# SwiGLU operands in two sets of tiles, six prepared weight blocks kept for the second half, output weight sums formed in the input stage

## The chip, the cores and the metric

The kernel runs on one core of one Trainium2 chip. TensorE (PE in the profile) multiplies matrices, VectorE (DVE), ScalarE (ACT) and GpSimd (POOL) work element by element, and SyncE (SP) issues the transfers between the main memory and the on-chip memory (SBUF). PE writes to eight PSUM banks, which DVE and ACT read. Every engine works through its own list of instructions strictly in that list's order and waits by semaphores for the others. The metric is the device time of one execution in microseconds; lower is better.

## The reference

One encoder layer works on 1280 tokens (1024 of a prompt and 256 of a sample) of width 1024: a mixer (differential attention beside a gated linear recurrence, the LRU), cross-attention into 2 x 256 memory tokens, and a SwiGLU of inner width 2816, each followed by a residual and a layer norm. The change lies in the SwiGLU, and in where some of its sums are formed:

```python
def swiglu(x, ffn_w_in, ffn_w_out):
    g, u = jnp.split(x @ ffn_w_in, 2, axis=-1)
    return (jax.nn.silu(g) * u) @ ffn_w_out

x = layer_norm(alpha*x + swiglu(x, ffn_w_in, ffn_w_out), ln3_g, ln3_b)
# mixer, the side products: sigmoid(g_attn) * (attn_out @ p_attn) + sigmoid(g_lru) * (lru_out @ p_lru)
```

## The kernel before

All matrix products are made of split operands: a float32 value is kept as a high part (a rounded copy) and a low part (the value minus the high part), and a product takes three matmuls: high by high, high by low, low by high. A **split** thus costs a copy on ACT and a subtraction on DVE or POOL (`split`, line 192).

The stages follow each other in time: input products with the LRU and the rotation of queries and keys (0 to 632 us of the span); attention with "filler" products between its steps (632 to 1395), the last of which are the side products with `p_lru`; `p_attn` and the mixer output (1395 to 1623); cross-attention (1623 to 1928); the SwiGLU (from 1928 on).

**First SwiGLU product.** Tokens are taken in two halves of 640. For each half 22 **units** f run, one for each block of 128 inner columns. A unit multiplies the gate block and the up block of weights by the tokens with a 7-product Strassen scheme (`strassen`, lines 359 to 391): seven products of 12 matmuls (4 steps of 3) of 320 columns, 84 matmuls in all, each product into one PSUM bank, and eight small evacuations (one on ACT, seven on DVE). The 7 weight operands of a unit are gate and up sub-blocks and four sums of them, each split in two: `pair_ops` (lines 328 to 349) loads both blocks (`raw`), forms the sums on DVE and POOL and splits. The gate pair goes to the pool `WT` (4 buffers of `wh` and `wl`), the other five pairs to `ws`, which has 5 buffers of each part, so one set. `P_ORDER` (line 357) uses the operands in the order 0, 5, 1, 6, 4, 2, 3; `pair_ops` writes operand 3 first of the five. Units 0 to 3 are **reloaded**: their operands were prepared during cross-attention and stand in main memory (`fpd`), and 14 transfers of 256 KB bring them in. I call the other 18 units **fresh**. The token operands `xb` are seven split combinations, one set for the half (`combine`, line 1129).

**Second SwiGLU product.** It is a Strassen scheme over inner halves and output halves, seven out-products (`out_product`, line 1266) of 11 steps of 15 matmuls of 512 columns. Product 0 runs between the two halves, product 1 after the second half, then 4, 5, 2, 6 and 3. The left sums are formed in `sums` (second half, one DVE operation for units below 11, three from 11 on) and stored to `sd`; the weight sums in `weight_sums` (first half, units 1 to 11, four DVE operations) are stored to `td`. `inner` and `inner2` load a step's two sources and split them.

**Order.** A scheduler lays out each engine's list from the order in which the code is written, pool sizes and priorities (`high_priority` with a negative offset puts work later). SP's list holds all loads and stores, so that a store which waits for its source also holds back the loads behind it. Fillers are drawn by `fill(done)` as attention proceeds; all their products share one PSUM bank (`ps_m`, line 681).

```python
while filled[0] < upto:                       # fill, line 722
for j in range(5): ... combine(j, xf, ...)    # after out_product(0, ...), lines 1301 to 1306
```

Of the kernel before, what the change touches and what calls it, by code (L numbers as in the profile page):

```python
# [9 lines left out]
F32 = mybir.dt.float32  # L10
# [22 lines left out]
FDB = 1  # L33
MSTB = 4
# [10 lines left out]
RELOAD = 4  # L45
PREP = 100
# [48 lines left out]
WSB = 5  # L95
# [45 lines left out]
def encoder_layer_kernel(ctx: ExitStack, tc: tile.TileContext, i, y_out):  # L141
# [11 lines left out]
    def f32(ap):  # L153
        return ap.bitcast(F32)
# [28 lines left out]
    fpd = dt_("fpd", [RELOAD, 7, 2, 128, 512])  # L183
# [3 lines left out]
    sd = dt_("sd", [4, NF // 2, 128, 640])  # L187
    td = dt_("td", [NF // 2, 128, 4, 512])
    SA = {4: 0, 5: 1, 6: 2, 2: 3}
# [240 lines left out]
    with ExitStack() as es:  # L430
# [170 lines left out]

        steps = [(k, b) for b in range(8) for k in "xy"]
# [16 lines left out]
        for n, (kind, b) in enumerate(steps):  # L619
# [46 lines left out]
    with ExitStack() as es:  # L666
# [16 lines left out]
        def fillers():  # L683
# [14 lines left out]
            for c0, n in (CHUNKS[2], CHUNKS[0], CHUNKS[1]):  # L698
# [18 lines left out]
        anchor = [None]  # L717
# [103 lines left out]
        done = 0.0  # L821
        for u in range(len(units) + VLAG):
# [23 lines left out]
            fill(done)  # L846
# [276 lines left out]
    with ExitStack() as es:  # L1123
# [47 lines left out]
        with ExitStack() as es1:  # L1171
# [6 lines left out]
            def reloaded(f):  # L1178
                if f == 0:
                    gs = [RW.tile([128, 1024], F32, tag="raw", name="raw").bitcast(F32R) for t in "hl"]  # L1180
                else:
                    gs = [WT.tile([128, 1024], F32R, tag="w" + t, name="w" + t) for t in "hl"]
                u = [tuple(ws.tile([128, 512], F32R, tag=t, name="s" + t) for t in "hl") for _ in range(5)]
                w = [tuple(g[:, c * 512:c * 512 + 512] for g in gs) for c in range(2)] + u
                for n, _ in P_ORDER:
                    for m in range(2):
                        SP.dma_start(f32(w[n][m]), fpd[f, n, m])
                return w

            def hidden(half_, f):  # L1190
                w = reloaded(f) if f < RELOAD else pair_ops(i["ffn_in"][f], i["ffn_in"][NF + f], [ws.tile([128, 512], F32R, tag=t, name="s" + t) for _ in range(5) for t in "hl"], rx, E_W, E_S)
# [11 lines left out]
            def sums(f, h):  # L1203
                def summand(src):
                    z = sp.tile([128, 640], F32, tag="z", name="hz")
                    SP.dma_start(z, src)
                    return z

                def put(n, z):
                    SP.dma_start(sd[SA[n], f % NK], z)  # L1210

                if f < NK:
                    z = summand(hd[0, f])
                    V.tensor_tensor(z, z, h, ALU.subtract)
                    put(6, z)
                    return
                k = f - NK
                z = summand(hd[1, k])
                V.tensor_tensor(z, z, h, ALU.add)  # L1219
                put(4, z)  # L1220
                y = summand(hd[0, k])
                V.tensor_tensor(y, z, y, ALU.subtract)
                put(5, y)
                z = summand(hd[0, f])
                V.tensor_tensor(z, z, y, ALU.subtract)
                put(2, z)


            def weight_sums(k):
                lo, hi, sa, sb = (rx.tile([128, 2, 512], F32, tag="raw", name="so") for _ in range(4))  # L1230
                SP.dma_start(lo, i["ffn_out"][k].rearrange("p (c n) -> p c n", c=2))
                SP.dma_start(hi, i["ffn_out"][NK + k].rearrange("p (c n) -> p c n", c=2))
                t1, t2, t3, t4 = sa[:, 0], sa[:, 1], sb[:, 0], sb[:, 1]
                V.tensor_tensor(t1, lo[:, 1], lo[:, 0], ALU.subtract)
                V.tensor_tensor(t2, hi[:, 1], t1, ALU.subtract)
                V.tensor_tensor(t3, hi[:, 1], lo[:, 1], ALU.subtract)
                V.tensor_tensor(t4, hi[:, 0], t2, ALU.subtract)
                SP.dma_start(td[k, :, 0:2, :], sa)
                SP.dma_start(td[k, :, 2:4, :], sb)
# [4 lines left out]
            def sources(n, k):  # L1244
                a = ASRC[n](k) if n in ASRC else sd[SA[n], k]
                b = BSRC[n](k) if n in BSRC else td[k, :, TB[n], :]
                return a, b
# [6 lines left out]
            def inner(n, k):  # L1254
                a, b = sources(n, k)
                return (parts(a, RW.tile([128, 1024], F32, tag="raw", name="raw")[:, :640], *(WT.tile([128, 1024], F32R, tag="w" + t, name="a" + t)[:, :640] for t in "hl")),
                        parts(b, rx.tile([128, 2, 512], F32, tag="raw", name="rb")[:, 0], *(ws.tile([128, 512], F32R, tag=t, name="b" + t) for t in "hl")))
# [30 lines left out]
            for half_ in range(2):  # L1288
                for f in range(NF):
# [6 lines left out]
                    if half_:  # L1296
                        sums(f, h)
                    elif 1 <= f <= NK:
                        weight_sums(f - 1)
                if half_ == 0:  # L1300
                    out_product(0, evac0, inner)
                    operands()
                    for j in range(5):
                        xf = rx.tile([128, 8, 128], F32, tag="raw", name="xf")
                        SP.dma_start(xf, x2t[:, :, j * 128:j * 128 + 128].rearrange("k p t -> p k t"))
                        combine(j, xf, rx.tile([128, 4, 4, 64], F32, tag="raw", name="tt"))
            out_product(1, evac1, inner)

        esx.close()
        with ExitStack() as es1:  # L1310
            ap_ = pool(es1, "a2", NK)
            rp = pool(es1, "raw2", 3)
            zp = pool(es1, "yb", 5)
            xt = pool(es1, "xt", 3)
            st = pool(es1, "stG", 2)
            gp = pool(es1, "gbF", 1)
            gt = gp.tile([128, D], F32, tag="g", name="lng")
            bt = gp.tile([128, D], F32, tag="b", name="lnb")
            SP.dma_start(gt, i["ln3_g"].partition_broadcast(128))
            SP.dma_start(bt, i["ln3_b"].partition_broadcast(128))  # L1320
            yb = []

            def inner2(n, k):
                a, b = sources(n, k)
                return (parts(a, rp.tile([128, 640], F32, tag="a", name="ra"), *(ap_.tile([128, 640], F32R, tag="a" + t, name="a" + t) for t in "hl")),
                        parts(b, RW.tile([128, 1024], F32, tag="raw", name="rb")[:, :512], *(ap_.tile([128, 512], F32R, tag="b" + t, name="b" + t) for t in "hl")))
# [9 lines left out]
            def normed(half_, p, y):  # L1336
                end = half_ == 1 and p == 4
                full = half_ == 1 and p >= 3
                with tc.high_priority(offset=0 if half_ else -LNP):
# [104 lines left out]
```

## Time and profile before

| | us |
|---|---|
| median of 3 runs | 2880.44 |
| lowest and highest | 2877.9, 2885.94 |
| profiled execution, whole | 2877.44 |
| its span, first to last instruction | 2875.6 |
| PE busy in the span | 2725.6 (95%) |
| DVE, ACT, POOL busy | 1753.2, 1205.3, 757.1 |
| mean granted clock of PE, share of full speed | 0.981 |

Busy time of PE counts matmuls that overlap, so that the length of a stretch, divided by the length of the same work without a wait, tells more. Idle time of the other engines matters only where PE waits for them.

### The profile page before, as it was taken

Reading aid. Unit: us, or ns where it says so; the run is one execution under the profiler, and the core shown is the slowest. Engines: PE = TensorE matmul, PEld = TensorE weight load, DVE = VectorE, ACT = ScalarE, POOL = GpSimd, SP = SyncE. Lnnn points to the kernel's source line nnn. Section 1 sums busy time; section 2 is a strip of 40 time slices with the busy share of each in tenths; the row PEclk is TensorE's granted clock in tenths of the full one; section 3 lists DMA queues with packets and bytes.
Section 4 is the critical chain, followed back from the end, with each engine's and each line's share of the span. In section 5 each row is a group of like instructions: output and inputs, shape, how many; then the busy total and the mean of one; then the engine's idle time right before and its main releaser. Section 6 shows DMA issues by size and latency. Waiting matters only on the chain. (4 is left out here: it accounts for less than half of the span.)

```text
span 2875.6 us, 40844 instructions
## 1 busy us (share of the span) xinstructions
PE 2725.6 (95%) x15075; PEld 2403.2 (84%) x15075; DVE 1753.2 (61%) x2567; ACT 1205.3 (42%) x2046; POOL 757.1 (26%) x491
## 2 busy tenths in 40 slices
PE   9999999999999999999999999999889789889898
PEld 7888888878899888888788899779889688888787
DVE  4546766416667655654355675556986457796568
ACT  3666445326666555554120254212333323333542
POOL 0000000014355443434001000322556245552004
PEclk9999999999999999999999999999999989999999
DMA  9533545574567756647786594669743663567654
GB/s 354 201 110 119 183 155 195 171 238 135 155 207 234 235 154 219 229 143 240 271 272 209 190 315 140 213 223 338 262 134 108 221 220 129 174 220 258 206 183 161
DMA packets 334792, 583.94 MB, mean 203 GB/s; under 512 B 27264, under 2 KB 170368, under 8 KB 334592
## 3 DMA queue, kind: packets, MB, share of 16 engines
q1 hardware_dynamic: 334592, 581.33, 60.9%
q8 instruction: 119, 1.95, 0.3%
q14 instruction: 81, 0.66, 0.1%
HBM read 389.33 MB, written 191.89 MB: 202 GB/s over the span
## 5 line engine op out<-in xcount | busy, mean ns | idle before, releaser
L197 POOL TENSOR_TENSOR wl<-raw,wh 128x1024 fp32r<-128x1024 f32 x88 | 213.2, 2424 | 913.0 <-ACT wh L194 865.2
L194 ACT ACTIVATE wh<-raw 128x1024 fp32r<-128x1024 f32 (+1 forms) x224 | 224.4, 1005 | 520.7 <-PE ps L293 152.3
L364 PE MATMUL ps<-xbh,sl 128*128 128x320 f32 x880 | 278.7, 317 | 41.4 <-DVE sl L197 41.0
L362 PE MATMUL ps<-xbh,sh 128*128 128x320 f32 x880 | 277.0, 315 | 23.8 <-ACT sh L194 13.9
L527 PE MATMUL ps<-xh,wh 128*128 128x512 f32 (+1 forms) x768 | 274.4, 357 | 11.3 <-ACT xh L194 6.1
L363 PE MATMUL ps<-xbl,sh 128*128 128x320 f32 x880 | 275.2, 313 | 0.0
L528 PE MATMUL ps<-xl,wh 128*128 128x512 f32 (+1 forms) x768 | 274.0, 357 | 0.5 <-DVE xl L197 0.5
L529 PE MATMUL ps<-xh,wl 128*128 128x512 f32 (+1 forms) x768 | 273.4, 356 | 0.0
L290 PE MATMUL ps<-fh,wh 128*128 128x512 f32 (+1 forms) x704 | 258.8, 368 | 10.8 <-DVE g L712 6.3
L293 PE MATMUL ps<-fl,wh 128*128 128x512 f32 (+1 forms) x704 | 255.6, 363 | 3.2 <-DMA fl<-memd 2.5
L197 DVE TENSOR_TENSOR wl<-raw,wh 128x1024 fp32r<-128x1024 f32 (+1 forms) x136 | 153.1, 1132 | 168.3 <-ACT wh L194 155.8
L294 PE MATMUL ps<-fh,wl 128*128 128x512 f32 (+1 forms) x704 | 254.9, 362 | 0.0
L750 DVE TENSOR_REDUCE nm<-s 128x1 f32<-128x1024 f32 (+1 forms) x160 | 167.3, 1059 | 93.6 <-PE s L749 92.9
L857 POOL TENSOR_TENSOR rstd<-rstd,mhalf 128x1 f32<-128x1 f32 x30 | 37.0, 1233 | 687.5 <-DVE rstd L856 687.5
L364 PEld LDWEIGHTS ps<-xbh,sl 128*128 128x128 f32 x880 | 168.1, 191 | 49.3 <-DVE sl L197 48.8
L362 PEld LDWEIGHTS ps<-xbh,sh 128*128 128x128 f32 x880 | 168.0, 191 | 27.7 <-ACT sh L194 17.0
L752 ACT ACTIVATE e<-s,nm 128x1024 f32<-128x1024 f32 (+1 forms) x160 | 158.7, 996 | 57.8 <-DVE nm L750 55.9
L527 PEld LDWEIGHTS ps<-xh,wh 128*128 128x128 f32 x768 | 146.4, 191 | 33.4 <-ACT xh L194 6.1
L363 PEld LDWEIGHTS ps<-xbl,sh 128*128 128x128 f32 x880 | 168.1, 191 | 0.0
L528 PEld LDWEIGHTS ps<-xl,wh 128*128 128x128 f32 x768 | 146.3, 190 | 21.5 <-DVE xl L197 1.1
L529 PEld LDWEIGHTS ps<-xh,wl 128*128 128x128 f32 x768 | 146.1, 190 | 20.7
L290 PEld LDWEIGHTS ps<-fh,wh 128*128 128x128 f32 x704 | 133.3, 189 | 34.6 <-issue 4.5
(287 smaller groups left out, 7334.1 us busy)
## 6 DMA issues: line engine op xcount, KB each, us to landing
raw<-w_in SPq DMA_DIRECT2D x80, 512.0 KB
raw<-ffn_in SPq DMA_DIRECT2D x80, 512.0 KB
q<-qd SPq DMA_DIRECT2D x320, 64.0 KB
hd<-hh SPq DMA_DIRECT2D x44, 320.0 KB
hz<-hd SPq DMA_DIRECT2D x44, 320.0 KB
sd<-hz SPq DMA_DIRECT2D x44, 320.0 KB
ra<-sd SPq DMA_DIRECT2D x44, 320.0 KB
raw<-p_lru SPq DMA_DIRECT2D x24, 512.0 KB
```

The source lines that it names most:

```text
L194: S.activation(h, src, AF.Copy)
L197: leng.tensor_tensor(l, src, f32(h), ALU.subtract)
L290: ins = PE.matmul(ps, a, h, start=(k == 0), stop=False)
L293: PE.matmul(ps, a, l, start=False, stop=False)
L294: PE.matmul(ps, b, h, start=False, stop=(k == 7))
L362: PE.matmul(ps, w[n][0][:, ks], xb[m][0][:, k, :], start=(k == 0), stop=False)
L363: PE.matmul(ps, w[n][0][:, ks], xb[m][1][:, k, :], start=False, stop=False)
L364: PE.matmul(ps, w[n][1][:, ks], xb[m][0][:, k, :], start=False, stop=(k == 3))
L527: PE.matmul(ps, wh[:, ks], h[:, k, :], start=(k == 0), stop=False)
L528: PE.matmul(ps, wh[:, ks], l[:, k, :], start=False, stop=False)
L529: PE.matmul(ps, wl[:, ks], h[:, k, :], start=False, stop=(k == 7))
L750: V.tensor_reduce(nm[:, c:c + 1], ps[:, :nk], axis=AX.X, op=ALU.max, negate=True)
```

## The change

- **Two sets.** A fresh unit's operands go to `WT` (gate pair and a second pair `s12`) and to three of now 6 `ws` buffers. Each pool then holds the operands of two units. Reloaded units use the same places, and load two operands at a time where they stand side by side.
- **Six kept blocks.** Units 6, 9, 12, 15, 18 and 21 store their 14 operand parts to `fpd` in the first half, and are reloaded in the second.
- **Weight sums.** The four sums for each of 11 steps are formed on POOL in the input stage, after the steps in `SUMSAT`, in the tiles of the rotation (`tab`, `o`, `z`).
- **Left sums.** The operands of products 5 and 2 are no longer stored: products 4, 5 and 2 keep the 11 left blocks in SBUF (`xk`) and change them by one DVE subtraction a step. Sources are loaded two steps at a time.
- **Half boundary.** `operands()` and the `combine` calls for the second half are written ahead of product 0.
- **Side products.** `fill` leaves 6 side products until after the attention loop, and every second of these uses a PSUM bank of `ps_t`.
- The layer norm's `ln3` vectors move into `WT` tiles and are loaded at their first use.

```diff
-            fill(done)
+            fill(min(done, total - 5.4 * HELD))
+        anchor[1] = True
         fill(1e9)
...
-                    gemm_fm(ps_m, w, lru, lambda ps: V.scalar_tensor_tensor(g, g, 1.0, ps, ALU.add, ALU.mult), tag="m", after=anchor[0])
+                    late = anchor[1] and b % 2
+                    gemm_fm(ps_t if late else ps_m, w, lru, lambda ps: V.scalar_tensor_tensor(g, g, 1.0, ps, ALU.add, ALU.mult), tag="t" if late else "m", after=anchor[0])
...
+        def weight_sums(k):
+            lo, hi, z = (rot.tile([128, 2, 512], F32, tag=t, name="so") for t in ("tab", "o", "z"))
+            SP.dma_start(lo, i["ffn_out"][k].rearrange("p (c n) -> p c n", c=2))
+            SP.dma_start(hi, i["ffn_out"][NF // 2 + k].rearrange("p (c n) -> p c n", c=2))
+            G.tensor_tensor(z[:, 0], lo[:, 1], lo[:, 0], ALU.subtract)
+            G.tensor_tensor(z[:, 1], hi[:, 1], lo[:, 1], ALU.subtract)
+            G.tensor_tensor(lo[:, 0], hi[:, 1], z[:, 0], ALU.subtract)
+            G.tensor_tensor(hi[:, 0], hi[:, 0], lo[:, 0], ALU.subtract)
+            for n, t in ((4, z[:, 0]), (6, z[:, 1]), (5, lo[:, 0]), (3, hi[:, 0])):
+                SP.dma_start(td[TB[n], k], t)
...
+            if n in SUMSAT:
+                with tc.high_priority(offset=-SUMP):
+                    weight_sums(SUMSAT.index(n))
...
+            def fresh(half_, f):
+                s12 = [WT.tile([128, 1024], F32R, tag="w" + t, name="s12") for t in "hl"]
+                tiles = [z[:, c:c + 512] for c in (0, 512) for z in s12]
+                tiles += [ws.tile([128, 512], F32R, tag=t, name="s" + t) for _ in range(3) for t in "hl"]
+                w = pair_ops(i["ffn_in"][f], i["ffn_in"][NF + f], tiles, rx, E_W, E_S)
+                if half_ == 0 and f in SAVED:
...
+                            SP.dma_start(fpd[x, n, m], f32(w[n][m]))
...
+                    operands()
+                    for j in range(5):
...
+                        combine(j, xf, rx.tile([128, 4, 4, 64], F32, tag="raw", name="tt"))
+                    out_product(0, evac0, inner)
...
+                    a = raws(n, k, 0)
+                    if n == 5:
+                        V.tensor_tensor(xs_[k], xs_[k], a, ALU.subtract)
+                        a = xs_[k]
+                    elif n == 2:
+                        V.tensor_tensor(xs_[k], a, xs_[k], ALU.subtract)
+                        a = xs_[k]
```

**ACT in the last units of the first half.** L194 and L198 are the copies of splits, `sh`, `wh` and `s12` the high parts of one unit's operands; L149 and L153 are the first evacuation of a unit (`sg<-ps`). The numbers grow with the order in which tiles were asked for: before, `sh_21247` to `sh_21255` and `sg_21281` belong to one unit, the last; in the change, `wh_21282` and `sh_21270` to `sh_21276` belong to the last unit and `sg_21165` to the one ahead of it.

```order
L194 ACTIVATE sh_21255<-raw_21258 128x512
L194 ACTIVATE ah_21446<-raw_21445 128x640
L194 ACTIVATE sh_21247<-sf_21267 128x512
L194 ACTIVATE sh_21249<-sf_21267 128x512
L194 ACTIVATE sh_21251<-sf_21268 128x512
L1194 ACTIVATE sg_21142<-sg_21142 128x640
L194 ACTIVATE sh_21253<-sf_21268 128x512
L149 ACTIVATE sg_21281<-ps_21283 128x320
```

and in the changed kernel:

```order
L198 ACTIVATE wh_21282<-raw_21278 128x1024
L198 ACTIVATE sh_21276<-raw_21279 128x512
L198 ACTIVATE s12_21270<-sf_21288 128x512 x2
L198 ACTIVATE sh_21272<-sf_21289 128x512
L1246 ACTIVATE sg_21028<-sg_21028 128x640
L198 ACTIVATE sh_21274<-sf_21289 128x512
L153 ACTIVATE sg_21165<-ps_21167 128x320
```

Before, a unit's last splits stand right ahead of that unit's own first evacuation; now the splits of the next unit stand there.

**ACT at the half boundary.** `ah` and `bh` are the operands of product 0, `xbh` the token operands of the second half, L1283 the evacuation of product 0, and `sg_21316` the evacuation of the last unit of the first half.

```order
L194 ACTIVATE bh_21668<-rb_21667 128x512
L194 ACTIVATE ah_21662<-raw_21661 128x640
L194 ACTIVATE xbh_21713<-xf_21727 128x4x64
L194 ACTIVATE xbh_21715<-xf_21727 128x4x64
L194 ACTIVATE xbh_21717<-xf_21727 128x4x64
L1283 ACTIVATE y_21688<-o_21386 128x512
```

and in the changed kernel:

```order
L198 ACTIVATE bh_21606<-rb_21605 128x512
L153 ACTIVATE sg_21316<-ps_21318 128x320
L198 ACTIVATE xbh_21421<-xf_21435 128x4x64
L198 ACTIVATE xbh_21421<-xf_21456 128x4x64
L198 ACTIVATE xbh_21421<-xf_21477 128x4x64
L198 ACTIVATE xbh_21431<-tt_21437 128x4x64
```

Before, the first `xbh` follows the last operand of product 0; now it follows the third (of eleven) and the first evacuation of the last unit.

**SP in the input stage, changed kernel.** `raw<-w_in` are the loads of the input weights, `so` and `td` the loads and stores of the weight sums, `xrd` and `lwr` belong to the LRU.

```order
L609 DMA so_1589<-ffn_out 128x1024
L551 DMA xrd_67<-stage_1410 128x1280
L610 DMA so_1590<-ffn_out 128x1024
L281 DMA raw_2391<-w_in 128x1024
L616 DMA td_82<-so_1591 128x512
L452 DMA lwr_1273<-lru_w 128x512
L616 DMA td_82<-so_1591 128x512
L616 DMA td_82<-so_1589 128x512
L616 DMA td_82<-so_1590 128x512
L609 DMA so_1819<-ffn_out 128x1024
```

The rows on `so` and `td` are new here; the others stood in this queue before.

## Rows read from the trace of the kernel before

**Rows 1.** Windows of stages: us, busy us (instructions) per engine, PEclk, DMA share, GB/s
```profile
0.00:530.00 530.00, 513.79 (x2635) 439.26 (x2636) 310.72 (x425) 285.54 (x376) 0.20 (x4) 1.00 0.52 184
...
1360.00:1395.00 35.00, 29.67 (x121) 23.16 (x120) 13.24 (x14) 9.54 (x9) 2.52 (x2) 0.95 0.79 259
...
1928.00:2247.00 319.00, 285.03 (x1855) 279.46 (x1854) 232.52 (x320) 101.61 (x165) 151.42 (x94) 0.96 0.61 208
...
2285.00:2303.00 18.00, 0.00 (x0) 0.00 (x0) 9.79 (x14) 8.08 (x23) 12.72 (x17) 0.55 0.79 236
...
2303.00:2627.00 324.00, 291.84 (x1848) 285.32 (x1849) 244.60 (x316) 102.78 (x171) 165.95 (x109) 0.94 0.57 198
...
2627.00:2868.00 241.00, 229.73 (x992) 187.95 (x990) 160.89 (x225) 94.21 (x142) 33.91 (x17) 0.98 0.59 193
```

**Rows 2.** Waits of all engines: total us, times, longest us
```profile
ACT sh L194 <- PE ps L363: 70.0, 37, 4.0
...
PE ps L364 <- DVE sl L197: 41.0, 28, 3.4
...
PE ps L362 <- ACT xbh L194: 23.5, 2, 18.5
...
PE ps L362 <- ACT sh L194: 13.9, 11, 6.5
```

**Rows 3.** Windows of single SwiGLU units and one output product
```profile
1927.60:1947.80 20.20, 15.30 (x95) 15.05 (x94) 8.16 (x16) 4.66 (x7) 0.92 (x1) 0.83 0.85 301
...
1960.20:1972.50 12.30, 12.30 (x86) 12.30 (x85) 4.89 (x10) 1.74 (x3) 1.57 (x1) 1.00 1.02 380
...
2151.50:2165.50 14.00, 12.66 (x86) 12.32 (x85) 9.47 (x13) 4.29 (x9) 8.36 (x5) 1.00 0.31 98
...
2303.20:2325.60 22.40, 16.67 (x84) 15.92 (x85) 10.59 (x14) 5.15 (x12) 13.59 (x17) 0.68 0.41 145
...
2753.00:2790.40 37.40, 37.40 (x166) 30.97 (x165) 24.66 (x38) 16.29 (x26) 0.00 (x0) 1.00 0.67 210
```

**Rows 4.** Timeline in a fresh unit: start, us, instruction, idle before it
```profile
2152.00 1.66 ACT L194 ACTIVATE sh<-sf 128x512 fp32r<-128x512 f32 x3
...
2154.07 0.97 DVE L197 TENSOR_TENSOR sl<-sf,sh 128x512 fp32r<-128x512 f32 x1
...
2155.09 0.42 PE L364 MATMUL ps<-xbh,sl 128*128 128x320 f32 x1 [1.34 <-DVE sl L197]
```

**Rows 5.** Lines by form, 1928 to 2247 us: busy us, mean ns, idle before
```profile
L197 DVE TENSOR_TENSOR sl<-sf,sh 128x512 fp32r<-128x512 f32 x36 | 44.4, 1235 | 1.9 <-ACT sh L194 1.7
...
L1235 DVE TENSOR_TENSOR so<-so 128x512 f32<-128x512 f32 x11 | 11.7, 1061 | 0.0
...
L391 DVE TENSOR_TENSOR cu<-ps,cu 128x320 f32<-128x320 f32 x21 | 10.2, 484 | 5.6 <-PE ps L364 5.6
...
L1237 DVE TENSOR_TENSOR so<-so 128x512 f32<-128x512 f32 x11 | 7.5, 680 | 0.0
...
L197 POOL TENSOR_TENSOR sl<-sf,sh 128x512 fp32r<-128x512 f32 x36 | 57.8, 1613 | 51.2 <-ACT sh L194 46.9 <-DVE sg L388 2.2 <-DVE sg L390 2.2
```

**Rows 6.** Lines by form, 2303 to 2627 us
```profile
L1214 DVE TENSOR_TENSOR hz<-hz,hh 128x640 f32<-128x640 f32 x11 | 17.8, 1621 | 5.8 <-POOL hh L1197 5.8
```

**Rows 7.** Chain that ended last, near the second stage-two product
```profile
2710.21 3.82 DMA rb<-td
...
2715.37 0.49 ACT yb L1348
```

**Rows 8.** Waits of PE from 1355 to 1395 us
```profile
PE ps L290 <- DVE g L712: 5.9, 5, 2.8
```

**Rows 9.** Page, part 5: costliest groups
```profile
L197 POOL TENSOR_TENSOR wl<-raw,wh 128x1024 fp32r<-128x1024 f32 x88 | 213.2, 2424 | 913.0 <-ACT wh L194 865.2
```

**Rows 10.** Timeline of the SP queue in the input stage
```profile
137.08 0.33 SPq L277 DMA_DIRECT2D raw<-w_in  x1
```

**Rows 11.** Timeline of ACT in the input stage
```profile
148.66 1.07 ACT L194 ACTIVATE wh<-raw 128x1024 fp32r<-128x1024 f32 x1
```

More of the change, by code (lines that the diff above doesn't have):

```diff
@@ L33 @@
 FDB = 1
+HELD = 6
 MSTB = 4
@@ L94 @@
 XMERGE = 1
-WSB = 5
+WSB = 6
 RXB = 6
@@ L1176, in encoder_layer_kernel, with weight_tiles @@
             st = pool(es1, "stF", 2)
[L1178 to L1185, printed above, removed]
-                    for m in range(2):
-                        SP.dma_start(f32(w[n][m]), fpd[f, n, m])
+            def weight_tiles(f=None):
+                g = [RW.tile([128, 1024], F32, tag="raw", name="raw").bitcast(F32R) if f == 0 else WT.tile([128, 1024], F32R, tag="w" + t, name="w" + t) for t in "hl"]
+                s12 = [WT.tile([128, 1024], F32R, tag="w" + t, name="s12") for t in "hl"]
+                return g, s12, [[ws.tile([128, 512], F32R, tag=t, name="s" + t) for t in "hl"] for _ in range(3)]
@@ new lines, in ordered, with both, two, reloaded @@
+            def ordered(g, s12, w):
+                wide = [[tuple(z[:, c:c + 512] for z in pair) for c in (0, 512)] for pair in (g, s12)]
+                return wide[0] + [w[1], w[2]] + wide[1] + [w[0]]
+            def both(x, n, m):
+                return fpd[x, n:n + 2, m].rearrange("n p c -> p n c")
+            def two(z):
+                return f32(z).rearrange("p (n c) -> p n c", n=2)
+            def reloaded(f, x):
+                g, s12, w = weight_tiles(f)
+                for pair, n in ((g, 0), (s12, 4)):
+                    for m in range(2):
+                        SP.dma_start(two(pair[m]), both(x, n, m))
+                for pair, n in zip(w, (6, 2, 3)):
+                    for m in range(2):
+                        SP.dma_start(f32(pair[m]), fpd[x, n, m])
+                return ordered(g, s12, w)
@@ L1188, in reloaded @@
                 return w
             def hidden(half_, f):
-                w = reloaded(f) if f < RELOAD else pair_ops(i["ffn_in"][f], i["ffn_in"][NF + f], [ws.tile([128, 512], F32R, tag=t, name="s" + t) for _ in range(5) for t in "hl"], rx, E_W, E_S)
+                if f < RELOAD:
+                    w = reloaded(f, f)
+                elif half_ and f in SAVED:
+                    w = reloaded(f, RELOAD + SAVED.index(f))
+                else:
+                    w = fresh(half_, f)
                 sg, cu = (st.tile([128, 2, 320], F32, tag=t, name=t) for t in ("sg", "cu"))
@@ L1203, in sums @@
             def sums(f, h):
[L1204 to L1239, printed above, removed]
+                z = sp.tile([128, 640], F32, tag="z", name="hz")
+                SP.dma_start(z, hd[int(f >= NK), f % NK])
+                V.tensor_tensor(z, z, h, ALU.add if f >= NK else ALU.subtract)
+                SP.dma_start(sd[SA[4 if f >= NK else 6], f % NK], z)
             ASRC = {0: lambda k: hd[0, k], 1: lambda k: hd[0, NK + k], 3: lambda k: hd[1, NK + k]}
@@ L1311, in encoder_layer_kernel @@
             ap_ = pool(es1, "a2", NK)
-            rp = pool(es1, "raw2", 3)
+            rp = pool(es1, "raw2", 2)
+            xk = pool(es1, "xk", NK - 8)
             zp = pool(es1, "yb", 5)
-            xt = pool(es1, "xt", 3)
+            xt = pool(es1, "xt", 2)
             st = pool(es1, "stG", 2)
[L1316 to L1319, printed above, removed]
@@ L1338, in normed @@
                 full = half_ == 1 and p >= 3
+                if not gb:
+                    for t, n in (("wh", "ln3_g"), ("wl", "ln3_b")):
+                        gb.append(f32(WT.tile([128, D], F32R, tag=t, name="ln" + t)))
+                        SP.dma_start(gb[-1], i[n].partition_broadcast(128))
+                gt, bt = gb
                 with tc.high_priority(offset=0 if half_ else -LNP):
```

59 lines of the change are left out of this document (45 added, 14 removed).

## Prediction

> **What bounds the kernel now.** I read the stage windows first, then the waits, then single units. PE is the bound nearly everywhere, so the question in each stage is how far its length lies above the same matmuls without a wait [rows 1]. A SwiGLU unit that never waits takes 12.3 us; a fresh one such as that at 2151.5 takes 14.0 [rows 3]. The two halves hold 22 units each, 22 x 12.3 = 271 us, and last 319 and 324 us: 48 and 53 us are lost. Between product 0 and the second half PE does nothing for 18 us (no matmul in that window). The last six out-products take 241 us against 6 x 37.4 = 224.4 of a product without a wait [rows 1, 3]: 16.6 lost. At the end of attention 5.3 of 35 us are idle. This makes 141 us that the change could reach; the rest of the program it only touches.
>
> The waits name the loss: PE waits 41.0 us for low parts (`sl`, 28 times), 13.9 for high parts, 23.5 for the token operands, and ACT waits 70.0 us with its `sh` copies for matmuls [rows 2]. One unit shows the loop: three copies run from 2152.00, DVE follows at 2154.07, and PE has waited 1.34 us at 2155.09, in the unit's second product [rows 4]. There is one set of five pairs; the first of them to be written is the last that the unit before reads, so all splits start only when that unit has ended, and the first product (12 of 84 matmuls) is too short to cover them.
>
> **First half, from 1928.** With two sets the splits of a unit belong to the time of the unit before it: in ACT's list they now stand ahead of that unit's first evacuation. The stall is gone as a rule of the code; what can remain is load. At 2151.5 the unit used 9.5 us of DVE and 8.4 of POOL [rows 3], 77% and 68% of 12.3 us. But the two slow each other: a 512-column split takes DVE 1.24 us on average, a subtraction of the same size that ran undisturbed 0.68 [rows 5]. So I leave 0.5 us of loss to each of the 18 fresh units (bounds 0 and 2.2, the latter from the first rival): 9 us. Unit 0 loses 20.2 - 12.3 = 7.9 now [rows 3]; its second product's operand moves to a pool that is free earlier, and I leave 3. The weight sums leave too, four operations of some 1 us in each of eleven units [rows 5], counted in the 0.5. 48 - 12: **gain 36**.
>
> The stores of six kept blocks hide beside this. A block is 14 x 256 KB = 3.67 MB; over three units with 1 MB of weights and 0.33 of results each that is 7.7 MB in 37 us, 208 GB/s, where the queue moved 380 in a unit that did not wait [rows 3].
>
> **The boundary.** Before, the first `xbh` stood in ACT's list behind the last operand of product 0; now the combinations start in the last unit and run beside product 0's 37 us. I leave 2 of 18 us (bounds 0 and 18): **gain 16**. What comes late next would be product 0's own operands, since ACT may hold them behind an `xbh` that waits for the last unit; three of eleven steps stand ahead of that.
>
> **Second half, from 2303.** Of the 53 us the first unit loses 10.1, at a granted clock of 0.68 of full speed, much of it at the lower of the two levels (1.2 instead of 2.4 GHz), after PE had stood idle for 18 us [rows 1, 3]; without the idle I leave 2. Ten units are now reloaded and need nothing of DVE but evacuations and one sum. Twelve fresh ones keep 0.5 each, 6 us. The sums cost DVE 1.62 us each under POOL's work [rows 6]; three per unit become one from unit 11 on. 53 - 8: **gain 45**. A reload costs 3.67 MB in 12.3 us, 298 GB/s, and the reloaded unit at 1960 did not wait with its queue at 380 [rows 3]; the mean over one kept and two fresh units is 8.7 MB in 37 us (3.67, two times 1.05, three times 0.98 of results and sums).
>
> **Output products.** In the second of them DVE and ACT waited on single loads of a right block (3.82 us, then a split), and ACT reached product 4's evacuation only at 2715.37 [rows 7]; PE idled there. Loads of two steps at a time halve these turns. Against it stand 22 more subtractions of 640 columns, 0.68 x 640/512 = 0.85 each, 18.7 us on a DVE that is busy 161 of 241 us [rows 1, 5], hidden under two products of 37.4; without that cover they would cost all 18.7. And the first left blocks now wait for tiles of product 1. I take half: **gain 8** (bounds -5 and 16.6).
>
> **Side products.** PE's list through the attention stage is the same row for row, so nothing is held back in fact; only the bank alternates. That removes five waits for `g`, 5.9 us together [rows 8]: **gain 5** (bounds 0 and 7, the latter with the clock).
>
> **Weight sums in the input stage.** 44 POOL operations, half of a 1024-column one of 2.42 us each [rows 9], are 53 us on an engine used for 0.2 of 530 us [rows 1]. On SP each sum adds six transfers, and the stores wait for POOL with the weight loads behind them. A weight load issued at 137.08 was first read at 148.66 [rows 10, 11], so some 11 us of delay are free. I take a **cost of 2** (bounds 0 and 137, see the third rival).
>
> **Sum.** 36 + 16 + 45 + 8 + 5 - 2 = 108 us. The profiled execution took 2877.4 us; 2769.4 follows. The median of the runs lies 3.0 above that execution, so I predict **2772 us**.
>
> **Rivals.**
> 1. *DVE and POOL become the bound.* If every operation of the one excluded those of the other, a fresh unit would need DVE's 5 x 0.68 + 1.36 + 7 x 0.484 = 8.1 us [rows 5] and POOL's 4 x 1.21 + 1.51 = 6.4 [rows 9] in a row, 14.5, so 2.2 over 12.3. With 18 units that is 40 instead of 9; in the second half, with a 0.85 sum, 3.0 x 12 = 36 instead of 6. Time 2772 + 61 = 2833, or 2803 if the reloaded units between give the second half's part back; the middle is 2818. For it: 1.24 against 0.68, and POOL's 1.61 against 1.21. Against it: evacuations keep 0.484 whatever POOL does, and at 2151.5 DVE had 4.5 of 14.0 us to spare. By the Trainium skill ("SBUF — State Buffer", section "SBUF: two separate sides") a DVE operation with two SBUF inputs and a POOL operation take one shared port pair as an exclusive lock, and the loser blocks for the whole instruction. By that rule the evacuations, with one input from PSUM, stay free, and the locked work is 4.8 + 6.4 = 11.2 us a unit, 91% of 12.3: PE would still set the pace, with little to spare. The durations in rows 5 lie between free and fully blocked.
> 2. *Kept blocks come late.* Their reads stand in SP's list behind stores that wait for a unit's end. If a block then lands at the 198 GB/s of the second half now [rows 1], it takes 18.5 us, 6.2 over, six times: 37 us, 2809. Against it: unit 1960 at 380 GB/s.
> 3. *Slower: the input stage starves.* A sum holds SP from its loads to its last store: a load of 3.82 [rows 7], four operations of 1.21, a store of 3.82, some 12.5 us, eleven times 137. Where two sums fall between two weight loads the 11 us are used up and PE waits. Time 2772 + 137 - 2 = 2907; it decides from about 110 us on. Against it: about one sum per input step of 14 us, and several weights are split ahead.
> 4. *The sets are not free in time*, the splits still wait for the unit before. Then 16 + 8 (the first unit's clock) + 8 + 5 - 2 = 35 remain: 2845.
>
> **How the numbers follow.** Forecast 0.74, rival 1 0.12, rival 2 0.06, rivals 3 and 4 0.04 each. A measurement of this kernel tells 0.3% (8.6 us) from no change. All but rival 3 lie below 2872: faster 0.95, same 0.02, slower 0.03 (the rest of rival 3 lands within). The low end has all of the 141 us gone but unit 0's 3 and some 8 of the output products, 130 off 2880, 2750; the high end takes in the middle of rival 1 and rival 2: 2818. The forecast's own range is 2750 to 2795.
>
> **What would show it.** Units of 12.3 to 12.8 us in both halves, and the `sl` wait below 10 us; no gap at the boundary, and a first unit of the second half below 15 us; no wait for `g` at the end of attention; a fresh unit's DVE work at 9.5 us or more in 12.5; the input stage still 530 us with POOL at some 55. I am wrong if fresh units stay at 14 us (rivals 1 or 4), if the kept units wait for `fpd` (rival 2), or if the input stage grows.

## The result, and the profile after

The changed kernel takes 2776.66 us (median; 2774.19 to 2780.24), the kernel before 2882.91 beside it: a ratio of 0.9634, 95% interval 0.9614 to 0.9654. Faster, 5 us above the forecast. The sum behind the forecast was less good than its end: one term was wrong by 27.5 us, and others made up for most of it. The profiled execution has a span of 2778.4 us against 2875.6, so 97.2 us are to be accounted for.

Windows of the changed kernel, borders at the same matmuls as in [rows 1] (columns as there): input stage, end of attention, first half, product 0, second half, the last six products.

```profile
0.00:559.50 559.50, 519.44 (x2635) 442.63 (x2636) 339.29 (x425) 285.87 (x377) 78.74 (x48) 0.97 0.62 216
1389.80:1416.80 27.00, 27.00 (x121) 22.37 (x120) 9.48 (x10) 7.44 (x7) 4.80 (x2) 1.00 0.88 292
1951.20:2225.50 274.30, 272.84 (x1860) 272.06 (x1859) 199.27 (x284) 111.22 (x183) 164.90 (x112) 1.00 0.67 235
2225.50:2262.90 37.40, 37.40 (x167) 30.95 (x166) 25.59 (x34) 15.88 (x33) 20.46 (x18) 1.00 0.82 270
2262.90:2539.90 277.00, 272.71 (x1849) 271.00 (x1848) 168.50 (x254) 78.07 (x126) 113.73 (x69) 1.00 0.70 250
2539.90:2768.10 228.20, 225.41 (x992) 185.47 (x990) 172.42 (x247) 92.78 (x143) 33.12 (x17) 1.00 0.58 199
```

Against [rows 1]:

| stage | before, us | after, us | gained | forecast |
|---|---|---|---|---|
| input stage | 530.0 | 559.5 | -29.5 | -2 |
| end of attention | 35.0 | 27.0 | 8.0 | 5 |
| first half | 319.6 | 274.3 | 45.3 | 36 |
| product 0 and the boundary | 56.0 | 37.4 | 18.6 | 16 |
| second half | 323.9 | 277.0 | 46.9 | 45 |
| last six products | 240.9 | 228.2 | 12.7 | 8 |
| all else (last stage 2.7 longer) | | | -4.8 | 0 |
| sum | | | 97.2 | 108 |

(The halves are taken from their first matmul to the next stage's, hence tenths off the windows of [rows 1].) A caution on single traces: in seven of the runs below the code of the second half is that of the change, and their traces show it at 271 to 279 us, the change at 277. The difference lies in the first unit and in units 12 to 18, so some 6 us there belong to no edit.

Three single stretches of the SwiGLU, for [rows 3]: unit 0, a fresh unit, the first unit of the second half.

```profile
1951.20:1966.70 15.50, 14.04 (x95) 13.26 (x94) 6.64 (x14) 4.42 (x7) 0.92 (x1) 1.00 0.83 278
2065.30:2077.60 12.30, 12.30 (x86) 12.30 (x85) 12.09 (x17) 5.18 (x8) 7.93 (x6) 1.00 0.26 102
2262.90:2276.00 13.10, 12.61 (x86) 12.34 (x85) 4.08 (x9) 2.98 (x5) 0.00 (x0) 1.00 1.04 386
```

A fresh unit takes 12.3 us even while DVE is busy for 12.09 of them; before it took 14.0. And PE's waits in the whole kernel after (total us, times, longest us), for [rows 2] and [rows 8]:

```profile
PE psl L474 <- ACT xch L198: 27.1, 5, 10.2
...
PE ps L366 <- DVE sg L388: 3.4, 2, 1.7
...
PE ps L366 <- DMA sh<-fpd: 1.4, 1, 1.4
...
PE ps L294 <- DVE g L732: 0.2, 1, 0.2
```

The waits for `sl` (41.0 us) and `xbh` (23.5) are gone. Kept blocks (`fpd`) cost PE two waits of 0.2 us; the 1.4 us are those of unit 0 of the first half. One wait has grown large, from 4.3 to 27.1 us: `psl`, the gate matmuls of the LRU in the input stage, waits for `xch`, which ACT copies from the convolution `xc` that DVE makes. In the kernel before:

```profile
PE psl L470 <- ACT xch L194: 4.3, 3, 2.6
```

So where did 29.5 us of the input stage go? DVE in the stretch 193 to 205 us of the changed kernel, ahead of and within the longest of these waits (198.8 to 209.0), and POOL beside it (start us, us, then the instruction):

```profile
193.25 1.50 DVE L501 TENSOR_TENSOR i<-i 128x1284 f32<-128x1284 f32 x1
194.66 0.94 DVE L463 TENSOR_SCALAR xc<-xp,vec 128x1284 f32<-128x1284 f32 x1
195.52 2.65 DVE L503 TENSOR_TENSOR i<-i,y 128x1024 f32<-128x1024 f32 x2
198.09 2.57 DVE L465 SCALAR_TENSOR_TENSOR xc<-xp,vec,xc 128x1284 f32<-128x1284 f32 x1
200.59 2.28 DVE L201 TENSOR_TENSOR wl<-raw,wh 128x1024 fp32r<-128x1024 f32 x1
202.79 2.55 DVE L465 SCALAR_TENSOR_TENSOR xc<-xp,vec,xc 128x1284 f32<-128x1284 f32 x1
```

```profile
196.49 1.40 POOL L611 TENSOR_TENSOR so<-so 128x512 f32<-128x512 f32 x1 [11.35 <-DMA so<-ffn_out]
197.85 1.46 POOL L612 TENSOR_TENSOR so<-so 128x512 f32<-128x512 f32 x1
199.28 2.51 POOL L613 TENSOR_TENSOR so<-so 128x512 f32<-128x512 f32 x1
201.86 2.12 POOL L614 TENSOR_TENSOR so<-so 128x512 f32<-128x512 f32 x1
```

DVE never idles in this stretch; it waits for no load (in run 1, below, for 0.45 us). While a weight sum runs on POOL, `xc` takes 2.57 us where an undisturbed one takes 1.55, `wl` 2.28 for 1.22. PE takes its list in order and stands at the gate matmul. Two theories:

- **A.** POOL's subtractions stretch DVE's operations, and DVE's LRU chain is what PE waits for in this stage.
- **B.** The 66 transfers of the sums (stores that wait for POOL in SP's list, or their share of the DMA) hold up loads.

### The profile page after: what moved, and what is told of

It reads as the page before. It is cut to its first block, busy times and chain, and to the rows that moved or that the text cites. A ratio compares the mean times of both kernels' runs of the same rounds, so it can differ in the third digit from the quotient of the medians.

```text
span 2778.4 us, 40821 instructions
## 1 busy us (share of the span) xinstructions
PE 2693.7 (97%) x15075; PEld 2383.7 (86%) x15075; DVE 1684.4 (61%) x2487; ACT 1185.2 (43%) x2010; POOL 799.3 (29%) x511
## 5 line engine op out<-in xcount | busy, mean ns | idle before, releaser
L198 ACT ACTIVATE wh<-raw 128x1024 fp32r<-128x1024 f32 (+1 forms) x218 | 218.3, 1005 | 398.3 <-PE ps L297 143.2
L366 PE MATMUL ps<-xbh,sh 128*128 128x320 f32 x528 | 163.4, 309 | 1.4 <-DMA sh<-fpd 1.4
L368 PE MATMUL ps<-xbh,sl 128*128 128x320 f32 x528 | 163.3, 309 | 0.1
L367 PE MATMUL ps<-xbl,sh 128*128 128x320 f32 x528 | 163.2, 309 | 0.0
L1283 PE MATMUL o<-bl,ah 128*128 128x512 f32 x385 | 150.2, 390 | 2.8 <-DVE bl L201 2.8
L297 PEld LDWEIGHTS ps<-fl,wh 128*128 128x128 f32 x704 | 133.0, 189 | 21.6 <-DMA fl<-memd 2.8
L298 PEld LDWEIGHTS ps<-fh,wl 128*128 128x128 f32 x704 | 132.8, 189 | 20.4
```

Source lines behind the costliest of these rows:

```text
L198: S.activation(h, src, AF.Copy)
L297: PE.matmul(ps, a, l, start=False, stop=False)
L298: PE.matmul(ps, b, h, start=False, stop=(k == 7))
L366: PE.matmul(ps, w[n][0][:, ks], xb[m][0][:, k, :], start=(k == 0), stop=False)
L367: PE.matmul(ps, w[n][0][:, ks], xb[m][1][:, k, :], start=False, stop=False)
L368: PE.matmul(ps, w[n][1][:, ks], xb[m][0][:, k, :], start=False, stop=(k == 3))
```

## Experiments

All are the changed kernel with the edit shown, unless said otherwise; ratios are to the kernel before, timed on the same chip.

**1. No subtractions.** The stores write the loaded halves, so this kernel leaves out the weight sums; the tile `z` goes too.
```
-            G.tensor_tensor(z[:, 0], lo[:, 1], lo[:, 0], ALU.subtract)   (and the three after it)
-            for n, t in ((4, z[:, 0]), (6, z[:, 1]), (5, lo[:, 0]), (3, hi[:, 0])):
+            for n, t in ((4, lo[:, 0]), (6, lo[:, 1]), (5, hi[:, 0]), (3, hi[:, 1])):
```


> The changed kernel without the four POOL subtractions of each of the 11 weight sums in the input stage; the two loads and the four stores of each stay (what is stored is the loaded halves, so the weight sums are not computed). Theory A (POOL's subtractions stretch the DVE operations of the LRU blocks beside them, and DVE's chain holds back the LRU gate matmuls in PE's list): the DVE forms of the stretch return to their lengths before (wl 1.22 us, xc 1.55, t 1.48), the three PE waits of 7 to 10 us go, the SwiGLU starts about 27 us earlier, and the time is 2750 us (2745 to 2757). Theory B (the sums' transfers: stores waiting in SP's queue ahead of the LRU's loads, or the share of the DMA engines): the waits stay and the time is 2777 us (2771 to 2781).

Measured: 2755.19 us, ratio 0.9531 (0.9506 to 0.9556). With all transfers in place the loss is gone. The same part of DVE's chain, in a slightly other order:

```profile
179.43 1.50 DVE L501 TENSOR_TENSOR i<-i 128x1284 f32<-128x1284 f32 x1
180.96 1.56 DVE L503 TENSOR_TENSOR i<-i,y 128x1024 f32<-128x1024 f32 x2
182.97 0.95 DVE L463 TENSOR_SCALAR xc<-xp,vec 128x1284 f32<-128x1284 f32 x1 [0.45 <-DMA xp<-xrd]
183.83 1.22 DVE L201 TENSOR_TENSOR wl<-raw,wh 128x1024 fp32r<-128x1024 f32 x1
184.97 1.55 DVE L465 SCALAR_TENSOR_TENSOR xc<-xp,vec,xc 128x1284 f32<-128x1284 f32 x1
```

**2. More of them.** Three of the four subtractions are written twice in a row.


> The changed kernel with three of the four POOL subtractions of each weight sum made twice (7 operations for 4, the same results and transfers). Theory A: the stretch of the DVE chain grows with POOL's work, by some three quarters of what it is now (27 us of longer DVE operations): 2797 us (2786 to 2805), with DVE's forms in the stretch longer in more places. Theory B: the transfers are the same and only the stores come later, by three POOL operations: 2777 to 2782 us.

Measured: 2796.77 us, ratio 0.9678 (0.9656 to 0.9700), some 13 us more than the change by the ratios (0.9678 - 0.9634, of 2890; the intervals leave 4 to 21). The direction is A's, and the 20 us that A expected lie at the edge. The 33 added operations lengthen DVE's by 14 us, the 44 of the change by 29 (table below), so they meet less of DVE. But theory B's mechanism is here too: the four stores of one sum, which wait for POOL, hold SP's list for 10.2 us, the rotation's table (`tab<-cos`) is issued behind them, and DVE waits 9.0 us for it. PE waits 7.8 us at 330.6 us for an evacuation with such a table (1.6 us in the change). SP's list, then DVE's:

```profile
295.69 10.20 SPq L616 DMA_DIRECT2D td<-so  x4
```
```profile
310.75 0.69 DVE L580 TENSOR_TENSOR rot<-ps,tab 128x512 f32<-128x512 f32 x1 [8.98 <-DMA tab<-cos]
```

**3. Subtractions that nothing waits for** (this kernel leaves out the weight sums as well).
```
-            G.tensor_tensor(lo[:, 0], hi[:, 1], z[:, 0], ALU.subtract)
-            G.tensor_tensor(hi[:, 0], hi[:, 0], lo[:, 0], ALU.subtract)
+            G.tensor_tensor(z[:, 0], hi[:, 1], z[:, 0], ALU.subtract)
+            G.tensor_tensor(z[:, 1], hi[:, 0], z[:, 0], ALU.subtract)
             (stores from lo and hi, as in 1)
```


> The run without POOL's sums left two readings open, since without the subtractions the stores in SP's queue no longer wait for POOL either. Here the four POOL subtractions of each weight sum run again, on the same loaded halves, but write only a tile that nothing reads, and the stores take the loaded halves (what is stored is not the weight sums): the stores do not wait for POOL. Theory A (POOL beside DVE stretches DVE's operations, and the LRU's chain on DVE holds PE): the DVE forms stay long, the PE waits for the LRU's gate operands stay near 27 us, ratio 0.961 to 0.965 (2777 us where the kernel before takes 2883). Theory B2 (the stores that wait for POOL hold up loads behind them in SP's queue): as without the sums, 0.953 to 0.956 (2750 us).

Measured: ratio 0.9596 (0.9579 to 0.9613), between the two expectations. The first two of the three large waits are there (9.6 and 10.0 us), the third (8.8 us in the change) is gone. DVE's lengths ahead of this third wait say why. In the change POOL subtracts from 242 to 265 us, and the scan of L499 takes 3.92 us; in this run no subtraction falls between 239 and 282 us, and it takes 2.83 (the change, then this run):

```profile
257.93 3.92 DVE L499 TENSOR_TENSOR_SCAN i<-r,t 128x1284 f32<-128x1284 f32 x1
```
```profile
251.41 2.83 DVE L499 TENSOR_TENSOR_SCAN i<-r,t 128x1284 f32<-128x1284 f32 x1
```

**4. The sums later in the same stage.**
```
-SUMSAT = (6, 7, 8, 9, 10, 11, 12, 13, 14, 15, 17)
+SUMSAT = tuple(range(18, 29))
```


> The changed kernel with the weight sums at steps 18 to 28 of the input stage in place of steps 6 to 17: the same POOL operations, transfers and tiles, later. The kernel before shows PE waits for the LRU's gate operands of 1.4 and 2.5 us at its second and third block and none after that, so the first blocks have no slack and the later ones may have some. Theory A with slack at the later blocks: POOL stretches DVE there as much, but PE does not wait: ratio to the kernel before 0.954 (2750 us where the kernel before takes 2883). Rival: the chain is as tight there, or SP's queue holds the loads with which attention begins: 0.963 (2777 us) or more.

Measured: ratio 0.9601 (0.9574 to 0.9628): by the ratios a third of the loss comes back, by the last gate matmul (table below) half. The later blocks have little slack: at 376.6 and 505.4 us PE waits 5.2 and 3.3 us, and DVE is lengthened by half as much as in the change, because the subtractions meet fewer of its operations (17 are longer, 28 in the change).

These runs in one table. *Stretch* is worked out from the traces: the sum, over every DVE instruction of the first 600 us, of its length less the median of its line and shape in the kernel before. The last gate matmul is the last instruction of line L474 (L470 before); the wait is that of `psl` for `xch`.

| kernel | DVE stretch, us | PE wait, us | last gate matmul, us |
|---|---|---|---|
| before | -0.1 | 4.3 | 511.2 |
| 1, no subtractions | -0.5 | 5.0 | 511.0 |
| 4, later | 14.7 | 13.8 | 525.7 |
| 3, not waited for | 24.1 | 20.6 | 527.6 |
| the change | 28.5 | 27.1 | 540.5 |
| 2, seven for four | 42.6 | 31.1 | 550.9 |

Both other columns rise with the stretch: the change stretches DVE by 29.0 us over run 1, and its last gate matmul comes 29.5 us later; run 2 by 43.1 and 39.9 (the late table has a part in these); run 3 by 24.6 and 16.6; run 4 by 15.2 and 14.7. The five changed kernels make the same number of transfers of the same sizes. The trace of the change agrees: from 80 to 560 us no matmul waits for a transfer and no copy of a weight block for its load; of the LRU's weights (`lwr`) ACT's waits grow from 0.2 to 4.0 us. B is out as the main cause in the change. In run 3 part of the stretch was harmless. Its stores no longer wait for POOL, which moved the subtractions in time, and what that is worth by itself stays open.

**5. The sums back in the SwiGLU's first half, on DVE** (one part of the change undone; `weight_sums(f - 1)` at units 1 to 11, its three tiles from that stage's raw pool).


> The changed kernel with one part undone: the weight sums formed again on DVE in units 1 to 11 of the SwiGLU's first half, in that stage's raw tiles. By theory A and by theory B the input stage returns to its length before (28 us less). What is told apart is the first half of the SwiGLU. If the second set of tiles alone brought its units to 12.32 us: they stay there and the time is 2750 us (2745 to 2756). If the sums had to leave DVE as well (10.5 us of work in a fresh unit of 12.3, and 3.8 us of sums on top): 1 to 2 us more in each of 11 units, 2762 to 2772 us.

Measured: ratio 0.9632 (0.9596 to 0.9668), as the change. The input stage gave its 28 us back, and units 3 to 12 lost them again (unit 4, the first fresh one, 10 us of them); units 13 to 20 take 12.32 us each. Windows of units 0 to 3, unit 4, and units 5 to 12 (columns as above):

```profile
1925.60:1978.90 53.30, 51.17 (x348) 50.32 (x347) 23.99 (x44) 9.04 (x14) 5.86 (x4) 1.00 0.99 364
1978.90:2001.20 22.30, 14.97 (x86) 14.70 (x86) 20.85 (x23) 7.68 (x12) 13.65 (x8) 0.77 0.78 265
2001.20:2117.40 116.20, 103.94 (x674) 101.44 (x674) 111.78 (x134) 41.20 (x66) 72.92 (x42) 0.97 0.90 316
```

In units 5 to 12 DVE is busy 111.78 of 116.20 us: it is the bound. Unit 4 is another case: the units ahead of it leave DVE half idle at a DMA share of 0.99, as in run 7 below. So the sums had to leave this place, and where they went cost as much.

**6. The sums in the stage that merges the branches**, on POOL, in tiles of their own, one at every second step (11 of its 24).


> The changed kernel with the weight sums, still on POOL, formed in the stage that merges the branches (around 1390 to 1530 us), in three tiles of their own; POOL is idle there and DVE 40% busy. Theory A: the input stage returns to its length before, and the stretched DVE operations of the merge stage are hidden under PE: 2750 us (2746 to 2758). Theory B: the same 22 MB of transfers now fall into a stage in which the DMA share is already 0.82 to 0.94, so they cost there what they cost in the input stage or more: 2770 to 2790 us.

Measured: 2812.97 us, ratio 0.9739 (0.9711 to 0.9767), 30 us slower than the change. Behind the merge stage stands one long wait, here with its cause (waits from 1440 to 1680 us, then SP's timeline):

```profile
DVE z L931 <- DMA z<-xtok: 69.3, 7, 61.0
...
PE ps L898 <- DVE z L931: 45.7, 1, 45.7
```

```profile
1562.65 0.33 SPq L965 DMA_DIRECT2D so<-ffn_out  x1
1564.01 0.33 SPq L966 DMA_DIRECT2D so<-ffn_out  x1
1567.69 4.27 SPq L972 DMA_DIRECT2D td<-so  x4
1572.02 0.92 SPq L909 DMA_DIRECT2D z<-xtok  x2
```

The next stage's first residual rows (`z<-xtok`) stand in SP's list behind the loads and stores of all 11 sums, which go one after the other through one set of tiles. That is theory B's mechanism, in another place: the four stores of each sum wait for POOL, whose subtractions wait for the sum's loads, which wait for the stores of the sum ahead. A second set of tiles or another queue was not tried.

**7. The sums in the second half, on DVE.**
```
+                    if half_ and f in SUMSAT:          # units of the second half
+                        weight_sums(SUMSAT.index(f))
-SUMSAT = (6, 7, 8, 9, 10, 11, 12, 13, 14, 15, 17)
+SUMSAT = (1, 2, 3, 5, 6, 8, 9, 11, 12, 15, 18)
```


> The changed kernel with the weight sums formed on DVE in the second half of the SwiGLU, at units 1, 2, 3, 5, 6, 8, 9, 11, 12, 15 and 18: seven of these are units whose blocks are loaded ready from memory, one or two of the others stand beside such a unit. DVE is busy 168.5 of 277 us there (61%), and 11 sums of 3.8 us make it 76%, against 73% in the first half, whose units hold 12.32 us. Theory A: nothing is lost there and the input stage gets its 28 us back: ratio 0.954 (2750 us where the kernel before takes 2883), at worst 0.957. Rival (the sums cost in the second half what they cost in the first, 28 us, because it is their transfers or their raw tiles that hold the units): 0.963 (2777 us).

Measured: 2763.69 us, ratio 0.9564 (0.9548 to 0.9580): three quarters of the gain that A expected. The input stage is as before the change to 3 us (last gate matmul at 513.8). In the second half units 2, 3 and 4 take 13.0, 15.0 and 21.3 us:

```profile
2261.90:2274.90 13.00, 12.51 (x86) 12.27 (x85) 5.48 (x10) 2.98 (x4) 1.55 (x1) 1.00 1.04 395
2274.90:2289.90 15.00, 12.78 (x86) 12.29 (x85) 6.58 (x12) 1.18 (x2) 1.58 (x1) 1.00 1.04 396
2289.90:2311.20 21.30, 14.47 (x87) 14.21 (x86) 18.87 (x19) 7.30 (x12) 15.84 (x9) 0.84 0.74 267
```

DVE is half idle in units 2 and 3, but the DMA share is 1.04. These are the loads of the reloaded units, and the sums' loads came on top; unit 4 is the first fresh one.

**8. The same at later units**: `SUMSAT = (5, 6, 8, 9, 11, 12, 14, 15, 17, 18, 20)`.


> As the run with the sums in the second half, at later units: 5, 6, 8, 9, 11, 12, 14, 15, 17, 18 and 20 in place of 1, 2, 3, 5, 6, 8, 9, 11, 12, 15 and 18. In that run units 2 to 4 lost 12.3 us of its second half (PE waiting for ACT's high part of an operand prepared afresh, 6.8 us once), units 5 to 21 only 3.7, and the DMA share of units 0 and 1 is 1.04 without any sum. Theory C (the sums' loads add to a DMA that is full while the kept blocks are loaded, and the raw blocks of the first fresh units come late): the loss at units 2 to 4 goes and the ratio to the kernel before is 0.952 (2751 us where the kernel before takes 2889), between 0.950 and 0.954. Rival (11 sums cost DVE and the raw tiles some 15 us wherever in this half they stand): 0.956.

Measured: 2748.40 us, ratio 0.9517 (0.9497 to 0.9537), as theory C had it. This version beats both kernels: by the ratios 34 us under the changed one (0.0117 of 2891), of which the traces show 29 in the input stage and 5 in the second half. Its input stage and second half:

```profile
0.00:530.50 530.50, 513.93 (x2636) 439.16 (x2637) 311.07 (x425) 286.09 (x377) 0.20 (x4) 1.00 0.53 184
...
2235.10:2507.10 272.00, 271.32 (x1849) 271.04 (x1848) 194.28 (x293) 76.59 (x122) 111.33 (x69) 1.00 0.92 335
```

Units 1 to 21 of this half take 12.32 us each, with DVE at 71%. The 3.4 us wait for `sg` of the change is gone too, which no theory had; it is absent in runs 1 and 3 as well, so the sums' new place is not shown to be the reason.

**9. Single parts undone.** No kept blocks (`SAVED = ()`):


> The changed kernel with one part undone: no prepared block is kept in the first half, so 18 of the 22 units of the second half are prepared afresh, as in the first. If two sets of tiles are what the units of 12.32 us rest on, the second half loses little: DVE goes from 168 to about 215 of 277 us, and the time is 2777 to 2787 us (ratio 0.963 to 0.967). If the kept blocks are needed (DVE's side sums on top of fresh units): fresh units of 13 to 13.5 us in place of 12.6, 2790 to 2800 us (0.968 to 0.971).

Measured: ratio 0.9726 (0.9711 to 0.9741), more than either expectation. Units 8 to 19 of the second half take 12.6 to 15.9 us. Window of these units (first unit 8's start to unit 20's), and its wait:

```profile
2365.10:2541.20 176.10, 156.75 (x1011) 152.57 (x1010) 139.58 (x169) 54.46 (x95) 109.37 (x62) 0.97 0.38 136
```
```profile
DVE sf L347 <- DMA raw<-ffn_in: 31.5, 11, 3.6
...
PE ps L366 <- DVE sg L388: 17.1, 11, 1.8
```

PE waits for a bank that DVE's evacuation has not left. DVE is busy for 79% of the window, and most of the rest it stands waiting for a raw block, whose load SP issues behind a store of results that waits for POOL. Whether DVE's load or this order is the cause was not separated. The six kept blocks are worth 27 us (0.0092 of 2889).

One bank for the side products held back (`late = False`):


> The changed kernel with one part undone: the six side products kept for the end of attention accumulate in one bank, as before, and not in two by turns. If the bank was what each waited for, the six waits of PE for DVE's g of the bank come back (6.1 us in the kernel before) and the end of attention gives back up to the 9 us that it gained: 2783 to 2786 us where the changed kernel takes 2777 (ratio 0.965 to 0.966). If keeping six products back until attention's last reads did it: no change, 0.963.

Measured: ratio 0.9648 (0.9628 to 0.9668), which the intervals alone don't tell from the change. The trace does: the six waits are back, and the end of attention takes 36.2 us for 27.0. The ratio shows less of it (4 us); in this trace the second half is 3 us shorter than in the change.

```profile
PE ps L294 <- DVE g L732: 7.3, 6, 3.7
```
```profile
1392.30:1428.50 36.20, 29.66 (x121) 23.15 (x120) 13.01 (x13) 10.60 (x10) 4.79 (x2) 0.95 0.80 246
```

Product 0 ahead of the combination again:


> The changed kernel with one part undone: the first output product stands ahead of the combination of the second half's tokens again, as before. If the 18 us that the boundary gained come from the product covering that combination: a gap of about 20 us without work for PE and a slower first unit behind it return, 2795 to 2803 us where the changed kernel takes 2777 (ratio 0.970 to 0.973). If the gain came from the second set of tiles (operands of the first unit loaded ahead): no change, 0.963.

Measured: ratio 0.9732 (0.9712 to 0.9752), 28 us: 21 at the boundary, and the first unit takes 20.6 us for 13.1. The wait of [rows 2] is back:

```profile
PE ps L366 <- ACT xbh L198: 24.0, 2, 20.5
```

**10. The kernel before with two sets of tiles alone.**


> The kernel before with one part of the change alone: the operands of a SwiGLU unit in two sets of tiles (and its kept blocks loaded in ten transfers). The weight sums stay on DVE in units 1 to 11, the side sums of the second half stay four a unit. If the set was what bound all units: both halves come to 12.4 us a unit and the time is 2883 - 90 = 2793 us (0.969). If DVE is the next bound where sums are formed (10.5 us of splits and 3.8 of sums against 12.3): the units with sums stay near 14 us and only the others gain: 2883 - 50 = 2833 us (0.983).

Measured: 2861.32 us, ratio 0.9904 (0.9884 to 0.9924): 28 us, where 50 and 90 were expected. The two halves:

```profile
1931.70:2235.40 303.70, 280.30 (x1859) 273.33 (x1857) 241.65 (x322) 100.88 (x166) 161.25 (x94) 0.98 0.63 216
...
2294.20:2608.20 314.00, 285.72 (x1849) 279.48 (x1850) 240.76 (x311) 97.55 (x168) 171.35 (x107) 0.96 0.56 195
```

In the first half units 13 to 21, which have no sums, take 12.3 to 13.1 us, units 4 to 12 up to 25.2. In the second, units 1 to 7 take 12.32 and most of units 8 to 19 14 to 17. The second set does remove the stall, and the full gain shows only in units that have no further sums. In units 8 to 19 of the second half DVE is busy for 83% of the time and waits 21.5 us for raw blocks, so here too its load and the order of the transfers are not told apart.

## Why the prediction was right, and where it was not

**First half** (36 forecast, 45.3 measured). The mechanism was right: with two sets a fresh unit needs no stall, and the 0.5 us left to each of 18 units was not needed. What I mis-sized is the part of the weight sums, put into that 0.5. Run 5 prices them at 28 us of the 45, 10 of these in unit 4. Rival 1 gave these fresh units 14.5 us; they hold 12.3 with DVE's low parts of 512 columns at 1.35 to 1.54 us on average (0.68 undisturbed), so overlap lengthens operations and yet fits. DVE does become the bound when some 4 us of sums stand in the same unit (run 5, units 5 to 12). With a side sum in each of 18 fresh units (run 9) the units are longer too, but DVE is not full there.

**Boundary** (16; 18.6) and **second half** (45; 46.9). In size as worked out. The first unit takes 13.1 us; no reloaded unit loses more than 0.8. Of the 6 us that the half loses, 4 stand in the fresh units 14 and 17, and not in every run; the forecast had 0.5 in each of twelve. Run 9 shows that the two terms rest on product 0's new place and on the kept blocks.

**Side products** (5; 8.0). The bank was the cause, not the holding back (run 9).

**Output products** (8; 12.7). Within the bounds; I had taken half of the loss, and three quarters of it went. The second of the six takes 40.3 us, the third to fifth 37.4 each, so the 22 added subtractions are mostly hidden. No run undoes this part, so what made the gain is argued and not shown:

```profile
2577.30:2617.60 40.30, 38.13 (x167) 30.84 (x167) 38.87 (x58) 20.02 (x33) 0.00 (x0) 1.00 0.67 225
2617.60:2729.80 112.20, 112.20 (x497) 92.94 (x496) 85.62 (x118) 51.40 (x80) 21.34 (x10) 1.00 0.57 197
```

**Weight sums in the input stage** (2 forecast, 29.5 measured): the step that failed. It read "44 POOL operations ... on an engine used for 0.2 of 530 us" as free room and priced only SP's list and the delay of weight loads. I had the stretch in hand, 1.24 against 0.68 in [rows 5], used it for the SwiGLU and did not ask which engine sets the pace where the sums were to go. The profile of before held the sign: PE waits there for `xch`, 4.3 us in three waits, small but with no slack behind them. Rival 3 had the right place and the wrong queue: no copy of a weight block waited for its load. The prediction's own sign of being wrong, a longer input stage, came true, and POOL is busy there for 78.7 us, where some 55 were expected.

By the Trainium skill ("SBUF — State Buffer", section "SBUF: two separate sides") a DVE operation with two SBUF inputs and a POOL operation exclude each other on one port pair. The trace agrees: a DVE operation of this kind that meets a subtraction is longer by about 1.0 us (1.55 to 2.57, 1.22 to 2.28), somewhat less than one undisturbed subtraction of 1.26, whatever its own length. The evacuations, with one input from PSUM, kept their 0.48 us, as in [rows 5] (lines by form, the first half of the changed kernel):

```profile
L395 DVE TENSOR_TENSOR cu<-ps,cu 128x320 f32<-128x320 f32 x21 | 10.1, 482 | 4.1 <-PE ps L368 4.1
```

**The total** came out within 5 us by luck: -27.5 here met +21.5 in the five other terms and -4.8 in stages that I had left at nothing, 10.8 short in all. By the medians only 4.7 of these are left, because the profiled execution of the kernel before lies 3.0 us under its median and that of the change 3.6 over its own.

## What to carry to other kernels

An idle engine is not free room if it slows another one beside it: before moving work to POOL, look for the stage in which DVE is not what PE waits for, not for the one in which POOL is idle. A small wait (here 1.4 and 2.6 us) that recurs at the same matmul can mark a chain without slack; here 29 us added to that chain cost the stage 29.5. And when transfers move with the work, look at the DMA share of the single units and at what stands behind them in the same queue: the same sums cost, by the ratios against run 8, 14 to 64 us more in five other places (runs 7, 4 and 5, the change, run 6).

## What the runs showed of the hardware that was not expected

- The stretch is nearly a fixed amount per meeting, about 1.0 us for a 512-column subtraction of 1.26 to 1.29 us (least and median in run 6), and does not grow with the DVE operation: `xcl` 0.69 to 1.76, `wl` 1.22 to 2.28, `xc` 1.55 to 2.57, a scan 2.82 to 3.80 us. In the change 28 DVE operations of this stage are lengthened, 24 of them by 0.9 to 1.1 us and none by more. Short operations suffer most. An operation with one SBUF input met it too: `xc`'s first (L463) takes 0.94 us and twice 1.9 in run 3.
- POOL pays as well: the third subtraction of a sum took 2.14 us on average in the change.
